# A decoder trunk of two layers on one core: the tile of the modulated input moves to another place in SBUF

## The chip, the cores and the metric

The kernel runs on one core of one Trainium2 chip. The metric is the device time of one execution in microseconds (us). The times of the kernel before are 2254.9, 2256.91 and 2256.86 us in three runs, median 2256.86 us.

The core has a matrix engine (TensorE, PE in the profile, its weight loads PEld), a vector engine (VectorE, DVE), a scalar engine (ScalarE, ACT), GpSimd (POOL) and a sync engine (SP), which issues nearly all DMA transfers. SBUF is the on-chip memory of 128 partitions that all of them read. PSUM holds the sums that PE writes.

## The reference

Two layers, each a token mixer followed by a gated feed-forward network with a short convolution. All inputs are float32, and there are 256 positions of width 2048.

```python
def reference(x, c, positions, ...):
    c_act = jax.nn.silu(c)
    for i in range(DEPTH):
        mod = c_act @ ada_w[i] + ada_b[i]
        sh1, sc1, g1, sh2, sc2, g2 = jnp.split(mod[:, None, :], 6, axis=-1)
        h = x * (1.0 + sc1) + sh1
        j = i // N_MIXERS
        if i % N_MIXERS == 0:
            y = fox_attention(h, fox_w_in[j], fox_b_f[j], fox_w_o[j])
        else:
            y = swa_attention(h, positions, swa_w_in[j], swa_sinks[j], swa_w_o[j])
        x = layer_norm(DEEPNORM_ALPHA * x + (1.0 + g1) * y, ln_mix_g[i], ln_mix_b[i])
        h = x * (1.0 + sc2) + sh2
        y = conv_ffn(h, ffn_w_up[i], ffn_conv_w[i], ffn_conv_b[i], ffn_w_down[i])
        x = layer_norm(DEEPNORM_ALPHA * x + (1.0 + g2) * y, ln_ffn_g[i], ln_ffn_b[i])
    return x
```

Each mixer projects `h` (`h @ w_in`), attends, and projects back (`o @ w_o`): layer 0 with a forgetting attention of 16 heads, layer 1 with a sliding window of 128, 32 query heads and 4 key heads. The feed-forward network is `u = h @ w_up` (2048 to 2 x 5632), a causal convolution of width 3 on `u`, `silu(g) * val`, and `@ w_down` (5632 to 2048).

## The kernel before, in words

**Numbers in halves.** A float32 matrix is split into a high half, rounded to the type that PE multiplies (`fp32r`), and the rest as a low half. A product is then three matmuls: high x high, high x low, low x high. The weights from HBM arrive in tiles `w` of two times 128 rows by 512 columns. ACT casts them to `wh` (line 264), DVE subtracts to get `wl` (line 275). There are 10 `w` tiles and 4 each of `wh` and `wl`, and each `wh` or `wl` is free again when PE has used it.

**The modulated input.** `h` is kept transposed and split in one tile, `hHL` (line 483): for each of 16 blocks `kc` of 128 input features the high half of all 256 positions, then the low half, so 2 KB a block and 32 KB a partition. It is written anew ahead of each of the four sub-layers (lines 503, 505, 84, 85). The output projections also use it: `o_tile` puts the attention's output of the last four of 16 blocks into `hHL`, while the earlier ones go to tiles of the general pool, called `oT`.

**Two ways to multiply.** A matmul loads 128x128 numbers into the array (its weight load) and streams a second tile past them. The profile writes `out<-in,in`, whichever of the two is moving.

- `x_mm` makes `x @ w` with the activations as the loaded operand and the weights `wh`, `wl` moving, 512 wide. It writes `xs`. It serves the value projection of layer 0 and the whole input projection of layer 1 (loaded from `hHL`, shown as `xs<-wh,hHL` and `xs<-wl,hHL`), the output projections (`oT`, and `hHL` for the last blocks) and the down projections (`gT`).
- `w_mm` and `u_mm` make the transposed product with the weights `wh`, `wl` loaded and `hHL` moving. `w_mm` (layer 0's queries and keys, written to `ws`) streams 256 columns three times. `u_mm` (the up projections, written to `us`) streams the high and low half together, 512 columns, past `wh`, and the high half, 256 columns, past `wl`.

**The pools.** All tiles lie in pools that are laid one behind the other in SBUF, in the order in which they are opened (lines 48 to 55): `cst` for single tiles, `wp` (`w` and other streams), `hl` (`wh`, `wl`), `gp` (30 general tiles of 2 KB: `gT`, `oT`, `qh`, `kT`, `pr` and others), `tp` and `sp` for temporaries. Inside `cst` the tiles lie in the order of their first use in the program. `hHL` is one of them; behind it come `stats`, the accumulator `acc`, `gate` and some small ones.

**The order of the work.** The streams of weights, the residual DVE work, and the background work (attention heads, modulation vectors of later sub-layers, convolution and gating) are put in an order by the program's own queues (`then`, `settle`, `defer`, `later`), and a scheduler places them on the engines. Attention heads and modulation vectors run between the matmuls of the streams.

Of the kernel before, what the change touches and what calls it, by code (L numbers as in the profile page):

```python
# [11 lines left out]
F32R = mybir.dt.float32r  # L12
# [5 lines left out]
P = 128  # L18
D = 2048
S = 256  # L20
NT = S // P
KC = D // P
# [19 lines left out]
def hybrid_trunk(ctx: ExitStack, tc: tile.TileContext, a: dict, out: bass.AP):  # L42
# [5 lines left out]
    cst = ctx.enter_context(tc.tile_pool(name="cst", bufs=1))  # L48
    wp = ctx.enter_context(tc.tile_pool(name="wp", bufs=10))
    hl = ctx.enter_context(tc.tile_pool(name="hl", bufs=4))  # L50
    gp = ctx.enter_context(tc.tile_pool(name="gp", bufs=30))
    tp = ctx.enter_context(tc.tile_pool(name="tp", bufs=4))
    sp = ctx.enter_context(tc.tile_pool(name="sp", bufs=4))
    psp = ctx.enter_context(tc.tile_pool(name="psp", bufs=8, space=bass.MemoryType.PSUM))
# [425 lines left out]
            ada_step()  # L480


    hHL = cst.tile([P, KC, 2, S], F32R, name="hHL")
    hH, hL = hHL[:, :, 0, :], hHL[:, :, 1, :]

    def mod_turn(k, n=1):
# [694 lines left out]
```

## Time and profile before

| what | value |
|---|---|
| median of 3 runs | 2256.86 us |
| profiled execution, its own time | 2256.56 us |
| its span (first to last instruction) | 2254.8 us |
| mean granted TensorE clock | 0.988 |
| matmuls into `us`, 512 and 256 wide | 2816 and 2816 |
| matmuls into `xs` with weights from `hHL` | 704 with `wh`, 352 with `wl` moving |
| matmuls into `xs` with weights from `gT` | 1408 with `wh`, 704 with `wl` moving |
| matmuls into `ws` | 1024 with `wh`, 512 with `wl` loaded |
| HBM traffic | 598.37 MB read, 266 GB/s over the span |

How to read it. Engines are given by busy time and number of instructions. A window is a stretch of the span with the busy time of each engine in it, the instruction counts in brackets, then the granted clock, the DMA share and GB/s. A group is a line, an engine, an operation, its tiles and shapes, the count, then busy time, mean duration in ns, and the idle time before it with the releaser. Matmuls are pipelined: the next begins while the last one still drains, so the durations of a group add up to more than the time it takes, and the pace is read from counts in a window. In the view of one tile a row has the smallest, median and largest duration. A wait has the total, the number and the longest.

The span falls into the opening and layer 0's attention (to about 350 us its input projections, to 478 us its output projection), the feed-forward network of layer 0 (to 1220 us), layer 1's attention (to 1500 us), and its feed-forward network (to 2240 us).

### The profile page before, as it was taken

What the parts mean: (1) busy time and instruction counts of PE and PEld (TensorE: products, weight loads), DVE (VectorE), ACT (ScalarE), POOL (GpSimd) and SP (SyncE); (2) the same over time, 40 slices, a digit from 0 to 9 for tenths busy, and PEclk for the clock granted to TensorE, in tenths of its full rate; (3) what the DMA queues carried; (4) which work ended last, traced back from release to release, by engine and by line L of the source; (5) the groups of instructions that cost most, each with busy time, mean ns of one, the idle gap of its engine ahead of it and who ended that gap; (6) DMA issues with size and microseconds to landing.
All of it is one profiled execution on the core that took longest, in us unless ns stands there. A gap on an engine that the chain in (4) does not pass through costs nothing. (4 is left out here: it accounts for less than half of the span.)

```text
span 2254.8 us, 33096 instructions
## 1 busy us (share of the span) xinstructions
PE 2196.5 (97%) x12037; PEld 1901.8 (84%) x12037; DVE 1847.4 (82%) x2626; ACT 1220.7 (54%) x2073; POOL 22.6 (1%) x52
## 2 busy tenths in 40 slices
PE   6999999999999999999999999999999999999997
PEld 5999888878888888888887788778888888888886
DVE  6979999979989968799888999769988655676766
ACT  3435656555555543655634588746555533555542
POOL 0000000000000000000000000000000000000000
PEclk9999999999999999999999999999999999999999
DMA  9999999958978989789887777648887555555553
GB/s 336 385 357 345 356 354 325 332 190 302 322 266 296 323 299 336 263 288 317 275 311 283 243 244 244 219 163 263 287 270 257 190 192 195 189 193 188 188 195 112
DMA packets 274228, 602.66 MB, mean 267 GB/s; under 512 B 21062, under 2 KB 29960, under 8 KB 273552
## 3 DMA queue, kind: packets, MB, share of 16 engines
q1 hardware_dynamic: 273008, 595.85, 76.5%
q0 software_dynamic: 1056, 4.69, 0.6%
q8 instruction: 94, 1.54, 0.3%
q14 instruction: 70, 0.57, 0.1%
HBM read 598.37 MB, written 2.10 MB: 266 GB/s over the span
## 5 line engine op out<-in xcount | busy, mean ns | idle before, releaser
L264 ACT CAST wh<-w 128x1024 fp32r<-128x1024 f32 x728 | 763.9, 1051 | 802.5 <-PE us L75 288.4
L275 DVE TENSOR_TENSOR wl<-w,wh 128x1024 fp32r<-128x1024 f32 x728 | 885.9, 1221 | 300.4 <-ACT wh L264 293.7
L75 PE MATMUL us<-hHL,wh 128*128 128x512 f32 x2816 | 985.7, 393 | 3.2 <-DVE hHL L505 3.2
L75 PE MATMUL us<-hHL,wl 128*128 128x256 f32 x2816 | 792.0, 283 | 3.2 <-DVE wl L275 3.2
L75 PEld LDWEIGHTS us<-hHL,wh 128*128 128x128 f32 x2816 | 530.2, 188 | 115.8 <-ACT hHL L503 3.9
L75 PEld LDWEIGHTS us<-hHL,wl 128*128 128x128 f32 x2816 | 534.4, 190 | 8.0 <-DVE wl L275 4.6
L75 PE MATMUL xs<-wh,gT 128*128 128x512 f32 x1408 | 435.7, 390 | 0.0
L75 PEld LDWEIGHTS xs<-wh,gT 128*128 128x128 f32 x1408 | 264.3, 188 | 54.8
L75 PE MATMUL xs<-wl,gT 128*128 128x512 f32 x704 | 273.9, 389 | 0.0
L75 PE MATMUL xs<-wh,hHL 128*128 128x512 f32 x704 | 238.5, 404 | 0.3 <-ACT wh L264 0.2
L404 DVE SCALAR_TENSOR_TENSOR acc<-wa,cact,acc 128x1024 f32<-128x1024 f32 x180 | 228.2, 1276 | 0.0
L75 PE MATMUL ws<-hHL,wh 128*128 128x256 f32 x1024 | 190.1, 288 | 4.4 <-ACT hHL L84 2.1
L75 PEld LDWEIGHTS ws<-hHL,wh 128*128 128x128 f32 x1024 | 162.0, 195 | 7.4 <-ACT hHL L84 2.7
L404 DVE SCALAR_TENSOR_TENSOR acc<-wa,cactp,acc 128x1024 f32<-128x1024 f32 x128 | 162.2, 1277 | 0.0
L75 PEld LDWEIGHTS xs<-wh,hHL 128*128 128x128 f32 x704 | 131.8, 190 | 30.0 <-issue 1.0
L75 PEld LDWEIGHTS xs<-wl,gT 128*128 128x128 f32 x704 | 132.2, 188 | 27.3
L75 PE MATMUL ws<-hHL,wl 128*128 128x256 f32 x512 | 143.7, 288 | 2.2 <-DVE wl L275 2.2
L75 PE MATMUL xs<-wl,hHL 128*128 128x512 f32 x352 | 141.7, 403 | 1.5 <-DVE wl L275 1.4
L75 PE MATMUL xs<-wh,oT 128*128 128x512 f32 x384 | 124.9, 395 | 0.1
L1069 ACT ACTIVATE u<-us,ccol 128x256 f32<-128x256 f32 x176 | 98.1, 562 | 39.4 <-DVE us L1067 39.4
L75 PEld LDWEIGHTS ws<-hHL,wl 128*128 128x128 f32 x512 | 98.4, 195 | 2.9 <-DVE wl L275 2.8
L1070 DVE SCALAR_TENSOR_TENSOR u<-us,ccol,u 128x255 f32<-128x255 f32 x176 | 83.3, 478 | 13.4 <-ACT u L1069 13.3
(217 smaller groups left out, 1753.3 us busy)
## 6 DMA issues: line engine op xcount, KB each, us to landing
w<-in_ffn_w_up_dram SPq DMA_DIRECT2D x352, 512.0 KB, 4.6
wa<-in_ada_w_dram SPq DMA_DIRECT2D x320, 512.0 KB, 5.4
w<-in_ffn_w_down_dram SPq DMA_DIRECT2D x176, 512.0 KB, 3.9
w<-in_fox_w_in_dram SPq DMA_DIRECT2D x96, 512.0 KB, 7.0
wo<-in_ada_w_dram SPq DMA_DIRECT2D x48, 512.0 KB, 9.3
w<-in_swa_w_in_dram SPq DMA_DIRECT2D x40, 512.0 KB, 5.6
w<-in_fox_w_o_dram SPq DMA_DIRECT2D x32, 512.0 KB, 5.5
w<-in_swa_w_o_dram SPq DMA_DIRECT2D x32, 512.0 KB, 5.3
```

Of the source, the lines that this page charges most:

```text
L75: return nc.tensor.matmul(o, lhsT, rhs, start=start, stop=stop, **kw)
L264: pin(nc.scalar.copy(h, w), False)
L275: pin(nc.vector.tensor_tensor(l, w, f32(h), op=ALU.subtract), behind[0] > 0)
L404: pin(nc.vector.scalar_tensor_tensor(ac, wo, (cactp if row else cact)[:, k:k + 1], ac, op0=ALU.mult, op1=ALU.add), True)
L1069: nc.scalar.activation(u, pf, AF.Identity, bias=cw(CW, f), scale=cw(2, f))
L1070: nc.vector.scalar_tensor_tensor(u[:, 1:], pf[:, :S - 1], cw(1, f), u[:, 1:], op0=ALU.mult, op1=ALU.add)
```

## The change

A pool `hp` of one buffer is opened behind the general tiles, and `hHL` is taken from it instead of from `cst`.

```diff
     wp = ctx.enter_context(tc.tile_pool(name="wp", bufs=10))
     hl = ctx.enter_context(tc.tile_pool(name="hl", bufs=4))
     gp = ctx.enter_context(tc.tile_pool(name="gp", bufs=30))
+    hp = ctx.enter_context(tc.tile_pool(name="hp", bufs=1))
     tp = ctx.enter_context(tc.tile_pool(name="tp", bufs=4))
     sp = ctx.enter_context(tc.tile_pool(name="sp", bufs=4))
...
-    hHL = cst.tile([P, KC, 2, S], F32R, name="hHL")
+    hHL = hp.tile([P, KC, 2, S], F32R, name="hHL")
     hH, hL = hHL[:, :, 0, :], hHL[:, :, 1, :]
```

The places in the built program, in bytes from the start of each partition:

| tile | before | after |
|---|---|---|
| `x`, `ident`, `cact` and other tiles ahead of `hHL` in `cst` | 4,096 to 27,903 | the same |
| `hHL` | 27,904 to 60,671 | 181,216 to 213,983 |
| the rest of `cst` (`stats`, `acc`, `gate`, ...) | 60,672 | 27,904 |
| `w` (10 x 4 KB) | 78,816 | 46,048 |
| `wh` (4 x 4 KB) | 119,776 | 87,008 |
| `wl` (4 x 4 KB) | 136,160 | 103,392 |
| general tiles (30 x 2 KB) | 152,544 | 119,776 |
| `tp`, `sp` | 213,984 | the same |

## The prediction

> **What bounds the kernel now.** I read the totals first, then the clock, then who waits for whom, then the costliest groups.
>
> ```profile
> span 2254.8 us, 33096 instructions
> PE 2196.5 (97%) x12037; PEld 1901.8 (84%) x12037; DVE 1847.4 (82%) x2626; ACT 1220.7 (54%) x2073; POOL 22.6 (1%) x52
> PEclk9999999999999999999999999999999999999999
> ...
> ACT wh L264 <- PE us L75: 288.4, 256, 2.4
> ACT wh L264 <- PE xs L75: 238.3, 167, 3.1
> ```
>
> TensorE is busy for 97% of the span at a granted clock that is full almost everywhere. The longest waits in the feed point the same way: the cast that makes `wh` waits 288.4 us and 238.3 us for matmuls to give a buffer back. So the pace is that of the matmul stream, and what matters is the step from one matmul to the next.
>
> The means of the groups are durations, and matmuls overlap, so I get steps from windows that hold one kind of matmul without a break. Each matmul has one weight load (PEld), shorter than the step, so length divided by the count of loads is the step.
>
> ```profile
> core 0: us, PE busy (x) PEld busy (x) DVE busy (x) ACT busy (x) POOL busy (x), PEclk, DMA share, GB/s
> 1250.87:1263.92 13.05, 13.05 (x57) 10.47 (x56) 13.02 (x21) 7.32 (x12) 2.76 (x3) 1.00 0.73 231
> 1470.41:1475.99 5.58, 5.58 (x25) 4.50 (x24) 2.74 (x3) 2.10 (x2) 0.00 (x0) 1.00 0.60 190
> 1475.99:1492.32 16.33, 16.33 (x73) 13.51 (x72) 10.57 (x12) 6.33 (x6) 0.00 (x0) 1.00 0.58 191
> 1492.33:1497.68 5.35, 5.35 (x24) 4.32 (x23) 2.26 (x4) 2.01 (x2) 0.00 (x0) 1.00 0.27 105
> 1800.00:1900.00 100.00, 100.00 (x443) 82.80 (x442) 52.27 (x49) 38.44 (x38) 0.00 (x0) 1.00 0.57 195
> 1920.00:2120.00 200.00, 200.00 (x1156) 177.31 (x1155) 140.59 (x213) 114.28 (x181) 0.00 (x0) 1.00 0.59 190
> 265.02:279.02 14.00, 14.00 (x121) 13.99 (x120) 14.00 (x14) 5.59 (x7) 0.00 (x0) 1.00 1.00 372
> 1505.92:1509.76 3.84, 3.84 (x13) 3.26 (x12) 2.83 (x4) 0.00 (x0) 0.00 (x0) 0.50 0.26 98
> ```
>
> The first row is the sliding-window input projection: 128x512 matmuls that stream `wh` or `wl` past weights loaded from `hHL`: 13.05/56 = 233.0 ns a step. The next three are one output projection, in order of time. Its middle takes its weights from general tiles (`oT`), 16.33/72 = 226.8 ns; before and behind it they come from `hHL`, which serves as `oT` for the last heads: 5.58/24 = 232.5 and 5.35/23 = 232.6 ns. Same line, same moving tiles, same shapes, no break between: what differs is the tile that the weights are loaded from. The fifth row is the down projection with weights from `gT`: 100/442 = 226.2 ns. So **a weight load from `hHL` costs some 6.2 ns a step more than one from a general tile**.
>
> The sixth row is the up projection, where `hHL` is the moving operand: a pair of one 512-wide and one 256-wide matmul every 2 x 200/1155 = 346.3 ns. The seventh is a 256-wide stream (`ws`, moving `hHL`): 116.7 ns. The last is the up projection at half the granted clock: 6 pairs in 3.84 us, 640 ns, which at full clock would be 320. So at full clock some 26 ns of a pair are neither clock nor wait; that part is open to whatever the places of the tiles do.
>
> **The change, part by part.** No instruction is added, removed or moved: the built program has the same instructions in the same order on all five engines, with the same waits, and the same DMAs in the same queues. Only places change. `hHL` starts at byte 27,904 of each partition before and 181,216 after. What was allocated behind it (`stats` to the columns, `acc`, `gate`, then `w`, `wh`, `wl` and the general tiles) lies exactly 32,768 bytes lower; the small tiles and the temporaries behind stay. A shift by 32,768 keeps the position modulo every smaller power of two, so among themselves `w`, `wh`, `wl` and `gT` stand as before. `hHL` alone changes: it starts at 256 modulo 512 before and at 480 after, and `wh`, `wl` and all general tiles are at 480 in both. In that respect `hHL` becomes one of the general tiles, and it also lies beside them. Either of the two could be what makes the quick step, and the trace can't separate them; both say the same of `hHL` as a weight tile.
>
> *Weights from `hHL`.* The counts, before and after 350 us:
>
> ```profile
> L75 PE MATMUL xs<-wh,hHL 128*128 128x512 f32 x224 | 75.1, 401 | 0.3 <-ACT wh L264 0.2
> L75 PE MATMUL xs<-wl,hHL 128*128 128x512 f32 x112 | 45.4, 407 | 1.5 <-DVE wl L275 1.4
> ...
> L75 PE MATMUL xs<-wh,hHL 128*128 128x512 f32 x480 | 163.4, 406 | 0.0
> L75 PE MATMUL xs<-wl,hHL 128*128 128x512 f32 x240 | 96.3, 401 | 0.0
> L75 PE MATMUL xs<-wh,oT 128*128 128x512 f32 x384 | 124.9, 395 | 0.1
> L75 PE MATMUL xs<-wl,oT 128*128 128x512 f32 x192 | 75.1, 391 | 0.0
> ...
> L75 PE MATMUL xs<-wh,gT 128*128 128x512 f32 x1408 | 435.7, 390 | 0.0
> L75 PE MATMUL xs<-wl,gT 128*128 128x512 f32 x704 | 273.9, 389 | 0.0
> ```
>
> The means of `oT`, in broken streams, lie 5 and 2 ns above those of `gT`: after a break the quick step isn't there at once. I therefore take 5.5 ns rather than 6.2. From 350 us on, 720 matmuls x 5.5 = 4.0 us. In the first 350 us the feed is at its limit too:
>
> ```profile
> 0.00:350.00 350.00, 323.67 (x2237) 299.65 (x2238) 301.75 (x381) 170.61 (x285) 12.14 (x37) 0.98 1.00 356
> 478.00:1220.00 742.00, 738.81 (x3936) 638.25 (x3935) 658.71 (x841) 398.87 (x639) 0.58 (x1) 1.00 0.86 298
> 1500.00:2240.00 740.00, 737.51 (x3907) 637.57 (x3908) 532.37 (x732) 383.51 (x549) 1.48 (x2) 0.99 0.63 209
> ```
>
> The DMA share there is 1.00, so I count half: 336 x 5.5 / 2 = 0.9 us. Together **4.9 us less**; ends: 0 (neither reason holds) and 1056 x 6.2 = 6.5. In the later windows DVE is busy for 659 of 742 us at most, so it can follow a feed that is needed half a per cent sooner.
>
> *`hHL` as the moving operand.* This is the larger lever, 2816 pairs, 2.8 us for each ns, and the part without a direct precedent: after the change moving and loaded operand both stand at 480. The nearest rows are moving general tiles:
>
> ```profile
> L75 PE MATMUL us<-hHL,wh 128*128 128x512 f32 x578 | 200.4, 390 | 0.0
> L75 PE MATMUL us<-hHL,wl 128*128 128x256 f32 x578 | 163.0, 282 | 0.0
> ...
> L75 PE MATMUL xs<-wh,gT 128*128 128x512 f32 x295 | 90.9, 389 | 0.0
> L75 PE MATMUL xs<-wl,gT 128*128 128x512 f32 x148 | 57.6, 389 | 0.0
> ...
> L75 PE MATMUL xs<-wh,hHL 128*128 128x512 f32 x16 | 5.2, 395 | 0.0
> ...
> L75 PE MATMUL S<-qh,ql 128*128 128x256 f32 x16 | 4.5, 282 | 0.0
> L75 PE MATMUL S<-ql,qh 128*128 128x256 f32 x16 | 4.5, 281 | 0.0
> L75 PE MATMUL ws<-hHL,wh x1024: 274/280/582, 23.6 to 355.1; 128*128 128x256 f32 x171
> ```
>
> The first two are the up projection inside 1920 to 2120 us, the next two the down projection inside 1800 to 1900 us. The fifth is weights from `hHL` inside 1470 to 1476 us. A 512-wide matmul lasts 390 ns with `hHL` moving and 389 with operands that both stand at 480; a 256-wide one 282 and, among general tiles, 281 to 282. Durations of unbroken streams differ as their steps do (`hHL` 395, `gT` 389 for steps of 233 and 226). So I take 1 ns for the pair: **2.8 us less**. The upper bound of the cost is the slow step met above, 6.2 ns on the 512-wide or on both, 17.5 to 35 us more; the lower one stands with the third rival. The `ws` matmuls (median 280) would go to 281.5: 1536 x 1.5 = 2.3 us more, half of it behind the DMA: **1.1 us more**.
>
> *What lies behind `hHL`.* ACT and DVE read and write the shifted tiles at addresses equal modulo 32,768, and DMA writes `w` likewise: nothing. Without that cover, DVE near its limit would show it first.
>
> The Trainium skill speaks against any effect here. "TensorE: Matmul & The Clock Gate", section "Step-by-step: what each phase is for", gives PE two independent SBUF read ports and says that loading the next weights takes nothing from the running matmul. By that rule the time would stay at 2256.9. The rows at 1470 to 1498 us disagree: the step is 232.6 or 226.8 ns by the weight tile alone.
>
> **The sum.** The profiled execution took 2256.56 us, 1.8 outside its span, and 0.3 under the median of the runs, 2256.86. 2256.56 - 4.9 - 2.8 + 1.1 = 2250.0; on the median's scale **2250.3 us**.
>
> **The rivals.**
>
> *The up projection loses its quick step (slower).* Place: the 2816 pairs of the two up projections. The step depends on how the moving and the loaded operand stand to each other, not on a good or bad tile: `hHL` under moving `wh` is slow, moving `hHL` over `wh` is not. Moving it may then break the relation that now works. Price: 2816 x 6.2 = 17.5 us for the 512-wide form, less 4.9: 2269.5; for both forms 2287. It decides from 4.9/2816 = 1.7 ns a pair on. For it: the pair is the one place where the present placement is as quick as any. Against it: operands that both stand at 480 are exactly those of the quick `gT` stream.
>
> *Nothing changes.* The slow step would come from something that goes with `hHL` but not with its place, say which instructions stand around it. For it: no instruction changes. Against it: the three rows of one output projection. 2256.9.
>
> *The up projection gains much.* If the 256-wide stream is a measure: 320/3 = 106.7 ns would be its step by the clock alone, it takes 116.7, so 10.0 is added for each matmul, against (346.3 - 320)/2 = 13.2 in the pair. 3.2 x 5632 = 18 us less, and 4.9: 2234. Against it: `gT`, which already stands as `hHL` will, adds about 13 as well.
>
> **How the numbers follow.** Forecast 0.48, slower 0.31, nothing 0.11, large gain 0.10. Within 0.2% (4.5 us, about what a measurement of this kernel can tell from no change) falls the second rival and 0.03 of the forecast's case: faster 0.45 + 0.10 = 0.55, same 0.14, slower 0.31. The forecast's own range is 2244 to 2253. The range of 2233 to 2272 takes in the large gain and the slower case with the 512-wide form, and leaves out the case where both forms lose.
>
> **What would show it.** The output projection of layer 1 should lose its contrast: windows with `hHL` at 226 to 228 ns a step. In the input projection of the sliding-window layer likewise. The up projection's pair should lie between 344 and 346.3 ns; above 348 the slower rival is right, near 340 the third. Durations of ACT's and DVE's splits (1051 and 1221 ns) should stay; if they move, the places of `w`, `wh`, `wl` matter and my reading of the shift is wrong.
>
> ```profile
> L264 ACT CAST wh<-w 128x1024 fp32r<-128x1024 f32 x728 | 763.9, 1051 | 802.5 <-PE us L75 288.4 <-PE xs L75 238.3 <-DMA w<-in_ffn_w_down_dram 83.5
> L275 DVE TENSOR_TENSOR wl<-w,wh 128x1024 fp32r<-128x1024 f32 x728 | 885.9, 1221 | 300.4 <-ACT wh L264 293.7 <-DMA w<-in_ffn_w_down_dram 2.0 <-DMA wa<-in_ada_w_dram 1.5
> ```

## The result and the profile after

The changed kernel takes **2268.13 us** (median of 4 runs, 2266.34 to 2270.45) against 2256.89 us for the kernel before on the same chip: ratio 1.0057, 95% interval 1.0044 to 1.0070. It is slower by half a per cent. The forecast was 2250.3 us; the slower rival had been priced at 2269.5.

First the totals, the two costliest splits and the matmul groups that the prediction spoke of, from the page of the changed kernel. Its line numbers are one higher than before.

```profile
span 2264.6 us, 33096 instructions
PE 2205.7 (97%) x12037; PEld 1900.8 (84%) x12037; DVE 1848.1 (82%) x2626; ACT 1220.0 (54%) x2073; POOL 25.4 (1%) x52
...
L265 ACT CAST wh<-w 128x1024 fp32r<-128x1024 f32 x728 | 764.0, 1051 | 813.6 <-PE us L76 305.8
L276 DVE TENSOR_TENSOR wl<-w,wh 128x1024 fp32r<-128x1024 f32 x728 | 886.9, 1223 | 308.3 <-ACT wh L265 295.0
L76 PE MATMUL us<-hHL,wh 128*128 128x512 f32 x2816 | 996.3, 399 | 3.2 <-DVE hHL L506 3.2
L76 PE MATMUL us<-hHL,wl 128*128 128x256 f32 x2816 | 787.5, 281 | 2.9 <-DVE wl L276 2.9
```

The counts are the same, and ACT's and DVE's splits last as long as before (1051 and 1223 ns, before 1051 and 1221). What grew is ACT's wait for the up projection to give back a `wh` buffer, 288.4 to 305.8 us: the matmul stream is slower, and what feeds it waits longer.

Now windows of the changed kernel: the input projection of the sliding-window layer, the three parts of its output projection, four stretches of streams with `hHL` moving. The columns are those of the prediction's windows.

```profile
1257.81:1270.08 12.27, 12.27 (x55) 10.13 (x54) 12.23 (x21) 6.91 (x11) 4.87 (x2) 1.00 0.75 230
1476.10:1481.30 5.20, 5.20 (x24) 4.31 (x23) 2.43 (x3) 2.11 (x2) 0.00 (x0) 1.00 0.64 200
1481.76:1497.39 15.63, 15.63 (x70) 12.95 (x69) 10.17 (x12) 6.30 (x6) 0.00 (x0) 1.00 0.63 197
1497.86:1502.83 4.97, 4.97 (x23) 4.12 (x22) 1.99 (x3) 1.76 (x2) 0.00 (x0) 1.00 0.33 111
...
960.31:1110.12 149.81, 149.81 (x850) 129.84 (x849) 139.47 (x197) 86.17 (x137) 0.00 (x0) 1.00 0.86 295
1540.00:1740.00 200.00, 200.00 (x1154) 176.02 (x1153) 179.16 (x254) 116.41 (x181) 0.00 (x0) 1.00 0.84 278
1920.00:2120.00 200.00, 200.00 (x1134) 173.53 (x1133) 135.18 (x201) 108.91 (x170) 0.00 (x0) 1.00 0.58 187
...
266.59:280.98 14.39, 14.39 (x121) 14.39 (x120) 13.84 (x13) 5.62 (x7) 0.00 (x0) 1.00 1.00 362
```

Read them by length over count of loads. With weights from `hHL` the step is now 12.27/54 = 227.2, 5.20/23 = 226.1 and 4.97/22 = 225.9 ns, as quick as the middle from `oT` (15.63/69 = 226.5): the contrast of before is gone, as forecast. The up projection went the other way: a pair takes 2 x 149.81/849 = 352.9 ns in layer 0 and 2 x 200/1133 = 353.0 in the same 200 us of layer 1 that gave 346.3 before. But at 1540 to 1740 us, in the same form at the same places, it takes 2 x 200/1153 = 346.9: the slow pace isn't forced by the places alone. The `ws` stream takes 14.39/120 = 119.9 ns, before 116.7.

The starts of some matmuls, read from the two traces, say where the time was lost (us from the start of the span; for the projections the matmuls with `wh`):

| first or last matmul of | before | after | later by |
|---|---|---|---|
| last `ws` | 355.2 | 357.3 | 2.1 |
| up projection of layer 0, first | 477.3 | 479.0 | 1.7 |
| up projection of layer 0, last | 1113.5 | 1120.8 | 7.3 |
| down projection of layer 0, last | 1223.4 | 1230.6 | 7.2 |
| up projection of layer 1, first | 1504.7 | 1510.1 | 5.4 |
| up projection of layer 1, last | 2132.2 | 2141.9 | 9.7 |
| last down projection | 2241.1 | 2250.9 | 9.8 |

The opening loses 2, the two up projections lose 5.6 and 4.3, the mixer of layer 1 gains 1.8, and the down projections don't move. The total is the difference of these two executions' spans, 2264.6 - 2254.8 = 9.8 us; the medians of the runs differ by 11.2.

### The profile page after: what moved, and what is told of

It is laid out like the page before. It is cut to its first block, busy times and chain, and to the rows that moved or that the text cites. A ratio compares the mean times of both kernels' runs of the same rounds, so it can differ in the third digit from the quotient of the medians.

```text
span 2264.6 us, 33096 instructions
## 1 busy us (share of the span) xinstructions
PE 2205.7 (97%) x12037; PEld 1900.8 (84%) x12037; DVE 1848.1 (82%) x2626; ACT 1220.0 (54%) x2073; POOL 25.4 (1%) x52
## 5 line engine op out<-in xcount | busy, mean ns | idle before, releaser
L265 ACT CAST wh<-w 128x1024 fp32r<-128x1024 f32 x728 | 764.0, 1051 | 813.6 <-PE us L76 305.8
L276 DVE TENSOR_TENSOR wl<-w,wh 128x1024 fp32r<-128x1024 f32 x728 | 886.9, 1223 | 308.3 <-ACT wh L265 295.0
L76 PE MATMUL us<-hHL,wh 128*128 128x512 f32 x2816 | 996.3, 399 | 3.2 <-DVE hHL L506 3.2
```

The lines of the kernel that those rows point to most:

```text
L76: return nc.tensor.matmul(o, lhsT, rhs, start=start, stop=stop, **kw)
L265: pin(nc.scalar.copy(h, w), False)
L276: pin(nc.vector.tensor_tensor(l, w, f32(h), op=ALU.subtract), behind[0] > 0)
```

## The experiments

**The place or the distance?** `e1_low_480` is the kernel before with two small tiles declared ahead of `hHL`: it stays among the low tiles, but starts at 28,128, which is 480 modulo 512. `e2_high_256` is the kernel after with three small tiles moved from `cst` into the new pool ahead of `hHL`: it stays behind the general tiles at 181,216, while `w`, `wh`, `wl` and the general tiles start 288 bytes lower, so that `hHL` stands to them as before. No instruction changes. The first from the kernel before, the second from the one after:

```diff
+    stats = cst.tile([P, NT, D // 512, nc.vector.BN_STATS_DIM], F32, name="stats")
+    mhalf = cst.tile([P, 1], F32, name="mhalf")
     hHL = cst.tile([P, KC, 2, S], F32R, name="hHL")
...
-    sint = cst.tile([P, NT, HR], F32, name="sint")
+    sint = hp.tile([P, NT, HR], F32, name="sint")
...
+    stats = hp.tile([P, NT, D // 512, nc.vector.BN_STATS_DIM], F32, name="stats")
+    mhalf = hp.tile([P, 1], F32, name="mhalf")
     hHL = hp.tile([P, KC, 2, S], F32R, name="hHL")
```

> hHL stays low in SBUF, where it was before, but 224 bytes further on (at 28,128, which is 480 modulo 512, as wh, wl and the general tiles are); stats and mhalf take the 224 bytes ahead of it, and nothing else moves. Theory R (what counts is how the loaded and the moving operand stand to each other modulo a small power of two, at most 512): all of the loss of the changed kernel is here too, about 2268 us; weights from hHL at about 227 to 229 ns a step, the pair of the up projection at about 351 ns, the 256-wide ws stream at 120 ns. Theory P (what counts is where in SBUF hHL or the weights lie): as before, about 2257 us, with steps of 233, 346 and 117 ns.

> hHL lies high, at 181,216 as in the changed kernel, and sint, stats and mhalf (288 bytes) have moved from cst to stand ahead of it, so that w, wh, wl and the general tiles lie 288 bytes lower still. hHL then stands 288 bytes modulo 512 past wh and wl, as in the kernel before. Theory R: the time of the kernel before, about 2257 us, weights from hHL at 233 ns, the pair at 346 ns, ws at 117 ns. Theory P: the time of the changed kernel, about 2268 us, with 227 to 229, 351 and 120 ns. If the remainder modulo 512 of each operand by itself counts, neither: all places modulo 512 but that of hHL are new.

Measured: `e1_low_480` 2269.67 us, ratio to the kernel before 1.0050 (1.0036 to 1.0064); `e2_high_256` 2255.24 us, 0.9995 (0.9986 to 1.0004). Windows of `e1_low_480` (up projection of layer 0, input projection of the sliding-window layer, up projection of layer 1), then of `e2_high_256` (the last two of these):

```profile
960.53:1110.33 149.80, 149.80 (x850) 129.88 (x849) 137.25 (x194) 86.41 (x143) 0.00 (x0) 1.00 0.85 292
1261.25:1273.55 12.30, 12.30 (x55) 10.13 (x54) 12.27 (x20) 6.86 (x11) 2.22 (x2) 1.00 0.72 226
1925.02:2124.99 199.97, 199.97 (x1133) 173.40 (x1132) 135.32 (x203) 110.56 (x172) 0.00 (x0) 1.00 0.57 186
```

```profile
1246.47:1259.05 12.58, 12.58 (x55) 10.13 (x54) 12.54 (x21) 7.19 (x12) 2.29 (x3) 1.00 0.75 232
1920.00:2120.00 200.00, 200.00 (x1156) 177.31 (x1155) 140.40 (x212) 114.65 (x181) 0.00 (x0) 1.00 0.58 190
```

`e1_low_480`, 153,088 bytes below the place of after, behaves as after: 2 x 199.97/1132 = 353.3 ns a pair, and 12.30/54 = 227.8 for the loaded step. `e2_high_256`, at the place of after, behaves as before: 346.3 and 12.58/54 = 233.0. So where `hHL` lies among the tiles makes no difference that these runs can tell. Nor does each tile's own remainder modulo 512: in `e2_high_256` `hHL` has that of after, `w`, `wh`, `wl` and the general tiles have a new one, and the times are those of before. What counts is the start of `hHL` against that of `wh`, `wl` and the general tiles. I call **distance** the start of `hHL` minus that of `wh`, modulo 256 bytes (the next run shows why 256): it was 32 before and in `e2_high_256`, and is 0 after and in `e1_low_480`.

**The distance by itself.** `e3_map` has the three forms of stream and nothing beside them: 64 pairs, then 96 matmuls with `hHL` loaded, then 192 narrow ones, for distances from 0 to 480 in steps of 32, and some at other absolute places. Its core:

```diff
+    for h, hd, wd in [("low", 0, 0), ("low", 0, 0), ("low", 32, 0), ("low", 64, 0),
...
+        for form in (pairs, loaded, narrow):
+            form({"low": low, "high": high}[h], hd // 4, wd // 4)
```

> Matmuls alone, nothing of the reference is computed (the output is a copy of x). For each distance of the activations from the weights, 0 to 480 bytes modulo 512 in steps of 32, it runs three streams of some 22 us: the up projection's pairs (activations moving, 512 and 256 wide), the 512-wide stream with the activations loaded, and the 256-wide ws stream; then two distances with the activations behind the weights instead of ahead of them, and three with other places modulo 512 at the same distance. Theory R: at distance 288 the steps of the kernel before (346 ns a pair, 233, 117), at distance 0 those of the changed one (351, 227, 120), whichever side the activations lie on and wherever the weights stand modulo 512, and some map over the other distances that repeats within 512. Theory P: steps don't depend on the distance, within 1 ns, and differ between the activations ahead and behind.

Windows at distance 0, 32 and 192, each with pairs, loaded, narrow. There is no column of DVE, which does nothing here; the others are in the same order, and the window holds as many steps as loads (one fewer than loads in the narrow form, whose loads touch):

```profile
core 0: us, PE busy (x) PEld busy (x) ACT busy (x) POOL busy (x), PEclk, DMA share, GB/s
91.85:108.45 16.60, 16.60 (x95) 14.40 (x94) 0.00 (x0) 0.00 (x0) 1.00 0.00 1
112.84:129.61 16.77, 16.77 (x75) 13.89 (x74) 0.00 (x0) 0.00 (x0) 1.00 0.00 1
133.26:153.41 20.15, 20.15 (x170) 20.15 (x169) 0.00 (x0) 0.00 (x0) 1.00 0.00 1
159.22:175.50 16.28, 16.28 (x95) 14.44 (x94) 0.00 (x0) 0.00 (x0) 1.00 0.00 0
179.94:197.20 17.26, 17.26 (x75) 13.89 (x74) 0.00 (x0) 0.00 (x0) 1.00 0.00 0
200.83:220.42 19.59, 19.59 (x170) 19.59 (x169) 0.00 (x0) 0.00 (x0) 1.00 0.01 2
...
496.79:513.39 16.60, 16.60 (x95) 14.43 (x94) 0.00 (x0) 0.00 (x0) 1.00 0.00 1
517.76:534.69 16.93, 16.93 (x75) 13.90 (x74) 0.00 (x0) 0.00 (x0) 1.00 0.00 0
538.25:557.28 19.03, 19.03 (x170) 19.03 (x169) 0.00 (x0) 0.00 (x0) 1.00 0.00 1
```

With PE alone at work the kernel's numbers come back: at 0 a pair 16.60/47 = 353.2, loaded 16.77/74 = 226.6, narrow 20.15/168 = 119.9; at 32 346.4, 233.2 and 116.6. So no other engine and no DMA is needed for it. What is left is PE's own work on the two tiles; that the moving tile of one matmul and the weights of the next get into each other's way is my reading, and no run here shows it by itself. The whole map, as mean steps in ns between the starts of matmuls behind the first 30 of each stream:

| distance | 0 | 32 | 64 | 96 | 128 | 160 | 192 | 224 |
|---|---|---|---|---|---|---|---|---|
| pair | 353.3 | 346.7 | 353.3 | 350.0 | 351.1 | 346.7 | 353.3 | 353.3 |
| loaded | 226.7 | 233.3 | 233.3 | 234.2 | 232.2 | 233.3 | 228.9 | 233.3 |
| narrow | 120.0 | 116.7 | 117.8 | 120.0 | 120.0 | 117.3 | 113.3 | 118.3 |

From 256 to 480 the same numbers return in the same order, and the tile behind the weights gives what the one ahead of them gives. The three forms don't agree on a best distance: **0 is the best for the loaded form and, in its slow pace, one of the worst for the pair.** For at 0 the pair has two steady paces: the very first stream, also at 0, ran at 346.7, as did one with both tiles 32 bytes further; so did the stretch of after at 1540 to 1740 us. The same stretch is quick in two more kernels with the networks at 0, `e1_low_480` (the first row) and `m_ffn_0` (the second, described next):

```profile
1540.00:1740.00 200.00, 200.00 (x1153) 175.97 (x1153) 179.51 (x255) 116.51 (x181) 0.00 (x0) 1.00 0.83 276
1540.00:1740.00 200.00, 200.00 (x1151) 175.76 (x1150) 181.33 (x257) 116.80 (x182) 0.00 (x0) 1.00 0.84 274
```

That is 2 x 200/1153 = 346.9 and 2 x 200/1150 = 347.8 ns. So there the pace isn't the chance of one execution. But which of the two a stream falls into, no run here explains.

**Which sub-layer.** A control, `c0_room`, gives `hHL` 256 bytes of room and lets a table set where in it each sub-layer's copy starts (the room comes from two small temporaries with two buffers instead of four). `m_ffn_0` puts the two feed-forward networks at distance 0 and leaves the mixers at 32; `m_mix_0` does the opposite; `m_best` takes the best of the coarse map for each: 192 for the mixer of layer 0, which is mostly narrow, 0 for that of layer 1, 32 for the networks.

```diff
+SHIFT = {("mix", 0): 0, ("ffn", 0): 0, ("mix", 1): 0, ("ffn", 1): 0}
...
-    hHL = cst.tile([P, KC, 2, S], F32R, name="hHL")
+    hall = cst.tile([P, KC * 2 * S + 64], F32R, name="hHL")
+    at = [SHIFT["mix", 0]]
...
+            v = hall[:, at[0] // 4:at[0] // 4 + KC * 2 * S].rearrange("p (k a s) -> p k a s", k=KC, a=2)
...
+        at[0] = SHIFT["ffn" if v else "mix", l]
```

The distance of a sub-layer is 32 plus its entry in `SHIFT`, modulo 256:

| kernel | `SHIFT` of mixer 0, network 0, mixer 1, network 1 |
|---|---|
| `m_ffn_0` | 0, 224, 0, 224 |
| `m_mix_0` | 224, 0, 224, 0 |
| `m_best` | 160, 0, 224, 0 |

> Control for the next three. hHL's tile gets 256 bytes of room at its end, what lies behind moves 256 bytes up, and two small temporaries have 2 buffers instead of 4 to make the space. hHL itself is used from offset 0, so its distance to wh, wl and the general tiles is 32 modulo 256 as in the kernel before. If the distance modulo 256 is all that counts (theory R, as the map showed it): 2256 us, within 0.15%. If places count otherwise, any other time.

> As the control, but the feed-forward networks use hHL from offset 224 of its tile (distance 0 modulo 256, as in the changed kernel), the mixers from offset 0 (32, as before). Theory R, with the map's steps: only the 2816 pairs change, from 346.7 to between 351 and 353.3 ns, 12 to 18.6 us more: 2268 to 2275 us. If the loss of the changed kernel came from elsewhere (the opening's ws stream, or DMA): under 2262 us.

> The other half: the mixers use hHL at distance 0, the feed-forward networks at 32. Theory R: 1056 matmuls with weights from hHL go from 233.3 to between 226.7 and 229 ns (4.5 to 7 us less), 1536 ws matmuls from 116.7 to 120 ns (5 us more, about half of it behind the DMA): 1 to 4.5 us less, 2251.5 to 2255 us. If the ws stream sets the opening's time in full: 0 to 2 us less.

> Each sub-layer at the distance that the map gives as its quickest: layer 0's mixer at 192 (ws 113.3 instead of 116.7 ns, weights from hHL 228.9 instead of 233.3), layer 1's mixer at 0 (226.7 to 229 instead of 233.3), the feed-forward networks at 32 (the pair at 346.7, as before). Theory R: layer 1's 576 matmuls 2.5 to 3.8 us less, layer 0's 480 some 2 us less, its 1536 ws matmuls up to 5 us less: 2245 to 2251 us, quicker than both kernels. If the opening goes at the pace of the DMA, only 2.5 to 4 us less, 2252 to 2254.

| kernel | median, us | ratio to before | 95% interval |
|---|---|---|---|
| `c0_room` | 2256.81 | 1.0006 | 0.9997 to 1.0014 |
| `m_ffn_0` | 2269.70 | 1.0063 | 1.0050 to 1.0077 |
| `m_mix_0` | 2254.93 | 0.9996 | 0.9987 to 1.0005 |
| `m_best` | 2252.36 | 0.9983 | 0.9974 to 0.9992 |

A window of the sliding-window layer's input projection and one of layer 1's up projection in `m_ffn_0`, then in `m_mix_0`:

```profile
1262.98:1275.57 12.59, 12.59 (x55) 10.14 (x54) 12.56 (x21) 7.18 (x12) 2.31 (x3) 1.00 0.75 228
1930.00:2130.00 200.00, 200.00 (x1134) 173.35 (x1133) 136.19 (x204) 110.61 (x175) 0.00 (x0) 1.00 0.64 187
```

```profile
1251.58:1263.85 12.27, 12.27 (x55) 10.13 (x54) 12.23 (x20) 6.88 (x11) 2.19 (x2) 1.00 0.73 216
1920.00:2120.00 200.00, 200.00 (x1156) 177.30 (x1155) 140.34 (x212) 114.53 (x181) 0.00 (x0) 1.00 0.65 190
```

`m_ffn_0` has the slow pair (353.0) and the slow loaded step (233.1); `m_mix_0` the quick pair (346.3) and the quick step (227.2). Against the control the networks at distance 0 cost 2269.70 - 2256.81 = 12.9 us, and the mixers at 0 give 1.9 us, which their interval alone can't tell from nothing. Together 11.0, and the change cost 2268.13 - 2256.89 = 11.2. So the whole loss lies in the up projections. `m_ffn_0` came out in the range of its expectation, `m_mix_0` where its two ranges meet. `m_best` missed the 2245 to 2251 us of its first expectation and came out at 2252.36, 4.5 us under the control, within the second, 2252 to 2254, in which the opening goes at the pace of the DMA.

**Is there a rule?** Three more kernels of matmuls alone. `e9_pairs` and `e10_loaded` take the distances to `wh` and to `wl` apart, eight of each in all 64 combinations; `e11_fine` goes from 0 to 64 in steps of 4 bytes.

```diff
-    for h, hd, wd in [("low", 0, 0), ("low", 0, 0), ("low", 32, 0), ("low", 64, 0),
+    for hd, wl in [(0, 0), (0, 0), (0, 224), (0, 192), (0, 160), (0, 128), (0, 96), (0, 64),
...
+    for hd, wl in [(0, 0), (0, 0), (4, 0), (8, 0), (12, 0), (16, 0), (20, 0), (24, 0), (28, 0),
```

> Matmuls alone, as in the first map: the up projection's pairs for all 64 combinations of the distance of hHL from wh and its distance from wl, each 0 to 224 modulo 256 in steps of 32. Theory R with the reads of the running and of the next matmul as the two sides: the 512-wide step depends on the distance to wl (its weights are loaded meanwhile), the 256-wide one on the distance to wh; equal distances repeat the first map, and the best combination may lie under 346 ns (340 if a 256-wide step of 113 and a 512-wide of 227 go together). If only the distance to one of them counts, rows or columns of the table are constant.

> The same 64 combinations for the stream with weights loaded from hHL and wh, wl moving, 512 wide. Theory R: 226.7 ns where both distances are 0, 233 to 234 where both are 32, 64, 96, 160 or 224, between them where the two differ; none under 226.

> All three streams at distances of 0 to 64 bytes in steps of 4. If the reads go in lines of 16 bytes (as the 16-byte cacheline of the Trainium skill, page SBUF - State Buffer, would have it), steps are the same within a line and change at multiples of 16; if in units of 32 or 64 bytes, they change there alone.

Two cells of `e9_pairs`, both 64 bytes from `wh`; the first is 0 from `wl`, the second 64:

```profile
403.72:419.69 15.97, 15.97 (x95) 14.17 (x94) 0.00 (x0) 0.00 (x0) 1.00 0.00 1
448.01:464.61 16.60, 16.60 (x95) 14.45 (x94) 0.00 (x0) 0.00 (x0) 1.00 0.00 1
```

15.97/47 = 339.8 ns against 353.2: it does matter how each of the two weight tiles stands. 339.8 is the lowest of the 64 pairs; the others lie between 346.5 and 353.4, and no row or column is constant. At (0, 0) both streams of `e9_pairs` ran at the quick pace, 346.7; in `e11_fine` the first stream at 0 ran at 346.7 and the second at 353.1. With the five of `e3_map` that makes five quick ones and four slow ones in nine streams at distance 0. Most cells of the three later kernels are a single stream, so a second pace there would not have shown. In `e10_loaded` only (0, 0) reaches 226.7; the others take 228.9 to 235.5. The fine map (mean steps in ns; the pairs at the places left out take 346.6 to 353.3, and at 0 the second stream is shown):

| distance | 0 | 4 | 12 | 16 | 20 | 24 | 28 | 32 | 36 | 60 | 64 |
|---|---|---|---|---|---|---|---|---|---|---|---|
| pair | 353.1 | 360.0 | 346.7 | 346.5 | 346.7 | 360.0 | 343.3 | 346.7 | 356.6 | 343.4 | 353.2 |
| loaded | 226.7 | 232.3 | 230.0 | 226.7 | 233.3 | 231.1 | 235.0 | 233.3 | 226.7 | 230.0 | 233.3 |

Its rows for the pairs at 24 and 28:

```profile
498.10:515.01 16.91, 16.91 (x95) 14.57 (x94) 0.00 (x0) 0.00 (x0) 1.00 0.01 1
566.12:582.24 16.12, 16.12 (x95) 14.25 (x94) 0.00 (x0) 0.00 (x0) 1.00 0.00 1
```

Four bytes change a pair from 16.91/47 = 359.8 to 16.12/47 = 343.0 ns. Steps of 16 or 32 bytes, which I had thought of as the unit, don't describe it. I found no rule that gives the numbers from the distances, so the map has to be measured.

**Does the map foretell the kernel?** If the distance is the cause, the two extremes of the fine map must show in the whole kernel. `m_28` is `m_best` with the networks at 28, 4 bytes lower; `m_24` is the control with the networks at 24.

```diff
-SHIFT = {("mix", 0): 160, ("ffn", 0): 0, ("mix", 1): 224, ("ffn", 1): 0}
+SHIFT = {("mix", 0): 160, ("ffn", 0): 252, ("mix", 1): 224, ("ffn", 1): 252}
...
+SHIFT = {("mix", 0): 0, ("ffn", 0): 248, ("mix", 1): 0, ("ffn", 1): 248}
```

> The kernel m_best with hHL 4 bytes lower in the two feed-forward networks, so that its distance to wh is 28 instead of 32 bytes modulo 256. Theory T (the step of a matmul at full clock is set by the distance between hHL and the weight tiles, and the matmul-only map carries over): the map has 343.3 ns for a pair at 28 and 346.7 at 32, so 2816 x 3.4 = 9.6 us less than m_best's 2252.4: 2242.8 us, ratio to the kernel before 0.994, and 343.3 ns for a pair in an unbroken stretch. Rival V (in the kernel, streams are broken by background work, and the transients after each break hide a difference of 3 ns): 2252.4 within 3 us.

> The control c0_room (every mixer at the old distance of 32) with the two feed-forward networks at a distance of 24 bytes modulo 256, 8 bytes lower. Theory T: the map has 360.0 ns for a pair at 24 against 346.7 at 32, so 2816 x 13.3 = 37.5 us more than the control's 2256.8: 2294.3 us, ratio 1.0166, and 360 ns for a pair in an unbroken stretch. Rival V (broken streams hide most of it, or the distance matters only in steps of 32 bytes): under 2270.

`m_28` takes **2243.90 us**, ratio 0.9946 (0.9932 to 0.9960); `m_24` 2286.97 us, 1.0138 (1.0123 to 1.0153). Windows of a part of layer 0's up projection and of both parts of layer 1's, in `m_28`:

```profile
950.00:1090.00 140.00, 140.00 (x817) 123.67 (x816) 133.35 (x190) 82.50 (x130) 0.00 (x0) 1.00 0.88 301
1520.00:1720.00 200.00, 200.00 (x1167) 176.63 (x1166) 181.38 (x259) 117.45 (x184) 0.00 (x0) 1.00 0.84 279
1900.00:2100.00 200.00, 200.00 (x1167) 176.68 (x1166) 139.97 (x210) 113.34 (x179) 0.00 (x0) 1.00 0.60 192
```

and of `m_24`, with a stretch at half the granted clock ahead of the second part:

```profile
970.09:1109.75 139.66, 139.66 (x778) 120.41 (x777) 127.58 (x180) 77.69 (x122) 0.00 (x0) 1.00 0.85 289
1520.65:1522.77 2.12, 2.12 (x8) 1.83 (x7) 2.12 (x4) 0.00 (x0) 0.00 (x0) 0.50 0.00 0
1545.24:1744.91 199.67, 199.67 (x1123) 174.31 (x1122) 176.62 (x253) 113.86 (x178) 0.00 (x0) 1.00 0.82 270
1940.15:2139.94 199.79, 199.79 (x1111) 172.31 (x1110) 133.20 (x200) 108.60 (x169) 0.00 (x0) 1.00 0.57 182
```

`m_28` runs at 2 x 200/1166 = 343.1 ns in both parts of layer 1, 343.1 in layer 0: the map's number. `m_24` runs at 359.5 and 360.0, and at 355.9 in the middle stretch, which again found another pace. Theory T asked for 2242.8 and 2294.3 us. The first holds within 1.1 us. Of the 37.5 us of the second 30.2 came (2286.97 - 2256.81), fewer than asked: the middle stretch is quicker, and what took the rest, the rival's broken streams or something else, no run here separates. The rival's limit of 2270 is far off. `m_28` beats both kernels of this case, by 0.5% and 1.1%, with the same instructions. The cell of 339.8 ns was not tried in a kernel: `wl` would have to start 64 bytes away from `wh`.

The row at half clock holds three pairs and one narrow step in 2.12 us. The starts of its matmuls give 640 ns for each of the pairs, as before the change and as in after and `m_28`. So the effect of the places shows only at full clock; at half clock four distances give the same step, in the 7 to 12 pairs that each of these traces has.

## Why the prediction was wrong

*What bounds the kernel*: right. The end moved by what the matmul stream lost; `m_28` and `m_24` moved it by 8.5 us down (from `m_best`) and 30.2 us up (from the control) through the pair alone. The remark that some 26 ns of a pair are open to the places was right too: the maps span 340 to 360 ns, 20 to 40 above the 320 that the prediction worked out for the clock.

*Weights from `hHL`*: the direction and the size of the clean step were right (233.0 to 227.2 ns), and both reasons given for it were named as inseparable; `e1_low_480` and `e2_high_256` separate them: it is the relation, not lying beside the general tiles. The mean was over-sized. By the starts of all matmuls with weights from `hHL` that follow one another without a gap, the mean step fell from 233.0 to some 229.0, 4 ns and not 5.5, since the many short streams don't settle at once: in the changed kernel the first four steps of a stream take 231.0 ns in the mean, the next four 229.3, and only those behind them 227. The mixers together gave 1.9 us (`m_mix_0` against its control), not the 4.9 less 1.1 of the forecast.

***`hHL` as the moving operand*: the step that failed.** I took 2.8 us less and it was 12.9 us more (`m_ffn_0`). Two links broke. First, I carried the quick stream of `gT` over to the up projection because "operands that both stand at 480" are common to both. The map shows that the same distance is quick in the one form and slow in the other: at 0, 226.6 ns loaded and 353.2 ns the pair. Even the quick pace of the pair at 0, 346.7 ns, gains nothing over before. What counts includes which operand moves, how wide it is and which weights come next, and `gT` moves nothing. Second, I read the step from durations, 390 against 389 and 282 against 281 to 282. Those rows compare matmuls of other operands and other orders; that durations follow steps within one form said nothing on what this form does at a new distance. The unknown was larger than any of those rows: the maps reach from 6.5 ns below the pair of before (339.8) to 13.5 above it (359.8), and the forecast put nearly half its chance on the side that an analogy named.

*The `ws` matmuls*: the direction was right, the size 3.2 ns instead of 1.5 (119.9 against 116.7). The start of the last one moved by 2.1 us, where 1.1 had been taken. (In this narrow stream the weight loads touch, 13.99 us of 14.00, so the prediction's "shorter than the step" does not hold for it; by the starts of its matmuls the step of before is 116.7 all the same.)

*What lies behind `hHL`*: right. `w`, `wh`, `wl` and the general tiles 32 KB lower cost ACT and DVE nothing, and `e1_low_480`, which shifts none of them by 32 KB, loses as much as the change.

*The slower rival* was right in mechanism and place: the relation that worked for the pairs was broken. It was priced at 6.2 ns for the 512-wide matmul and nothing for the other. By the starts of the matmuls, the step behind the 512-wide one grew by 5.6 ns in the mean and the one behind the 256-wide shrank by 1.5; of the long stretches only the one at 1540 to 1740 us, and a shorter one around 570 to 630, kept the quick pace. That its total came within 1.4 us is in part luck: it put the pairs at 17.5 us where they cost 12.9, and the gain of the mixers at 4.9 where it was 1.9, and the two errors largely cancel. Its argument against itself, the stream of `gT`, is the link that fell. *Nothing changes* fell with the windows, and with it the rule quoted from the Trainium skill ("TensorE: Matmul & The Clock Gate", section "Step-by-step: what each phase is for"): where that page has the next weights' load take nothing from the running matmul, a pair in `e11_fine`, with PE alone at work, takes 343 to 360 ns by the distance alone. *The up projection gains much* was wrong for distance 0, but a gain of its kind exists: at 28 the pair is 3.2 ns quicker than before.

## What to carry to other kernels

In this kernel, which its matmuls bound, the start of an operand against that of the weights, modulo 256 bytes, is a setting worth up to 5% of a stream's time (343 to 360 ns a pair), with no instruction added or removed. It can't be carried from one form of matmul to another, not even with the roles of the tiles exchanged: measure it for each form with a small kernel of that form alone, which takes some 22 us a place, more than once since a place can have two paces, and then place the operand, per sub-layer if need be. And whoever moves a tile for another reason should compare that distance before and after, as an unrelated small tile declared ahead can shift it.

## What the runs showed of the hardware

- At full granted clock a stream of these matmuls, each with its own weight load, takes 226.7 to 235.5 ns for 512 columns (`e10_loaded`) and 113.3 (`e3_map`, at 192) to 123.3 (`e11_fine`, at 4) for 256 by the places of its operands, with only PE at work. The coarse map repeats after 256 bytes, and a step of 4 bytes can change a pair from 359.8 to 343.0 ns. At half clock a pair takes 640 ns at the distances 0, 24, 28 and 32.
- Two starts in one line of 16 bytes need not give the same step. The Trainium skill ("SBUF — State Buffer", section "Specifications (TRN2)") gives SBUF cachelines of 16 bytes; 24 and 28 lie in the same one, with 359.8 and 343.0 ns.
- One distance can have more than one steady pace: 346.7 and 353.3 ns at 0, 355.9 and 360.0 at 24, each held over some 200 us of a kernel. What selects the pace, and what in the chip makes the distance count, stays open.
